# A 1024-token decoder block with PEER experts: down-projection sums over eight expert chunks instead of four

## The chip, the cores and the metric

The kernel runs on one core of one Trainium2 chip. The metric is the device time of one execution in microseconds (us), lower is better. A profiled execution gives the span from the first to the last instruction and the busy time of each engine: PE (TensorE, matrix products), DVE (VectorE), ACT (ScalarE), POOL (GpSimd) and SP (SyncE, which here only issues DMAs). 16 DMA engines move the data.

## The reference, cut to what matters

The block is an attention and convolution mixer, a layer norm, and then a PEER channel mixer with 16384 experts, which is where most of the time goes. For each of 1024 tokens, 8 heads choose 16 experts each; an expert is one row u of 1024 numbers and one row v of 1024 numbers:

```python
def chunk(args):
    xc, ec, gc = args                      # 128 tokens, their 128 experts, the gates
    u = jnp.take(u_experts, ec, axis=0)
    a = jax.nn.gelu(jnp.einsum('tkd,td->tk', u, xc), approximate=False)
    vv = jnp.take(v_experts, ec, axis=0)
    return jnp.einsum('tk,tkd->td', gc * a, vv)
# then h = layer_norm(DN_ALPHA * h + ff, ln2_g, ln2_b)
```

Summed over experts this is `(gates * gelu(h @ u.T)) @ v`, with a gate of zero for each expert that a token has not chosen.

## The kernel before, in words

The 1024 tokens are 8 blocks of 128. The experts are computed in two ways at the same time.

**Row blocks** (`ROWS`: 0, 1, 6, 7) fetch only the chosen rows. `gathered` issues, for each block, 128 indirect DMAs of u rows (L148) and 128 of v rows (L160), 128 rows of 4 KB each, so 1024 gathers of 512 KB in all. POOL issues them; they land in a pool of five buffers (`NGATHER`), shared by tag `t4k`. DVE consumes each with one instruction of 1024 columns (L150 a dot product, L162 a scaled sum in PSUM) and thereby frees the buffer.

**Dense blocks** (`DENSE`: 2 to 5, 512 tokens) compute all 16384 experts as 128 chunks (`NC`) of 128. `up(c)` loads 512 KB of u (L677), splits it into a high and a low part (ACT L120, DVE L121), runs 24 matmuls of 512 columns into one PSUM bank (L684), applies gelu on ACT (L689), multiplies by the gates on DVE (L690), and splits the product into `Wh` and `Wl`. The gates were written to DRAM earlier (`gd`); L687 fetches them for `QUAD` = 4 chunks at a time, 1 MB in pieces of 512 bytes, into two buffers `gq`. `down(q, jj)` loads 512 KB of v (L700), splits it with ACT and POOL (L121 on POOL), and for each of two slices j runs 12 matmuls (4 chunks, 3 products, L716) into a PSUM bank; DVE then adds the bank to `accT` in SBUF (L722; ACT copies it for q = 0, L720). All u and v loads go through four buffers with tag `raw`.

The loop at L755 walks the groups of chunks: first `up` of the first chunk of group q, then all the `down` steps of group q-1, then `up` of the other chunks of group q. After each of these units, `advance` traces a number of gather steps, so that all 1024 would be traced by nine tenths of the units. After the loop come the last group's `down` steps, cut into halves of 256 tokens with their layer norm (`finish`) behind each half (L773), and the remaining gathers. The framework's scheduler fixes the order of the instructions on each engine at build time from a timeline simulation, with priority by the order of the trace; on the chip each engine follows its order strictly.

Before the dense stage, mixer, routing keys and expert choice run for four pairs of blocks; some of the gathers already run there.

Of the kernel before, what the change touches and what calls it, by code (L numbers as in the profile page):

```python
# [13 lines left out]
F32 = mybir.dt.float32  # L14
F32R = mybir.dt.float32r
# [5 lines left out]
ALU = mybir.AluOpType  # L21
# [4 lines left out]
P = 128  # L26
T = 1024
D = 1024
NJ = D // P
# [16 lines left out]
ND = len(DENSE)  # L46
TD = ND * P
NMAX = max(len(g) for g in GROUPS) * P
NC = 128
QUAD = 4  # L50
TG = 32
OT = 8
HB = 64
GSCALE = 2.0 ** 15
NGATHER = 5
TK = 4
AHEAD = 8
NW = 5
EARLY = (3, 1)

WIDTH = [TOPK // (a + 1) for a in range(TOPK)]
# [16 lines left out]
def block_kernel(ctx: ExitStack, tc: tile.TileContext, d, out):  # L78
    nc = tc.nc
# [10 lines left out]
    gd = dram.tile([TD // TG, P, NC, TG], F32, name="gd")  # L90
# [92 lines left out]
    with ExitStack() as s1:  # L183
# [435 lines left out]
        n = p1.tile([P, NB, 8], F32, name="n")  # L619
# [18 lines left out]
        for gi, blocks in enumerate(GROUPS):  # L638
            x, qkv = xin
            y = p2.tile([P, NJ, NM], F32, name="y", tag="T", bufs=4)  # L640
            for b in range(2):
                a = scores(gi, b, qkv)
# [13 lines left out]
    with ExitStack() as s2:  # L656
# [15 lines left out]

        def up(c):

            q = c // QUAD
            raw = dn.tile([P, NJ, P], F32, name="uraw", tag="raw", bufs=4)
            nc.sync.dma_start(raw, d["uT"][c])  # L677
            uh = dn.tile([P, NJ, P], F32R, name="uh", tag="uh", bufs=2)
            ul = dn.tile([P, NJ, P], F32R, name="ul", tag="ul", bufs=2)
            split(uh, ul, raw)  # L680
            ps = pd.tile([P, TD], F32, name="pd")
            for j in range(NJ):
                for k, (w, z) in enumerate(((uh, 0), (uh, 1), (ul, 0))):
                    nc.tensor.matmul(ps, w[:, j], hT[z][:, j], start=(j == 0 and k == 0), stop=(j == NJ - 1 and k == 2))  # L684
            if q not in gq:
                gq[q] = dn.tile([P, TD // TG, QUAD, TG], F32, name="gq", bufs=2)
                nc.sync.dma_start(gq[q], gd[:, :, q * QUAD:(q + 1) * QUAD].rearrange("a p c t -> p a c t"))  # L687
            ge = dn.tile([P, TD], F32, name="ge", bufs=2)
            act(ge, ps, AF.Gelu)  # L689
            V.tensor_tensor(ge.rearrange("p (a t) -> p a t", t=TG), ge.rearrange("p (a t) -> p a t", t=TG),  # L690
                            gq[q][:, :, c % QUAD], op=ALU.mult)
            wh = dn.tile([P, TD], F32R, name="Wh", bufs=NW)
            wl = dn.tile([P, TD], F32R, name="Wl", bufs=NW)
            split(wh, wl, ge)
            W[c] = (wh, wl)

        def values_of(q, jj, tags=("vh", "vl")):

            raw = dn.tile([P, 2, QUAD, P], F32, name="vraw", tag="raw", bufs=4)
            nc.sync.dma_start(raw, d["vL"][q, jj])  # L700
            vh = dn.tile([P, 2, QUAD, P], F32R, name="vh", tag=tags[0], bufs=2)
            vl = dn.tile([P, 2, QUAD, P], F32R, name="vl", tag=tags[1], bufs=2)
            split(vh, vl, raw, G)
            return vh, vl

        def add(q, j, v, t0=0, n=TD):

            nonlocal accT
            if accT is None:
                accT = dn.tile([P, NJ, TD], F32, name="accT")  # L710
            vh, vl = v
            ps = pd.tile([P, n], F32, name="pd")
            for k in range(QUAD):
                wh, wl = W[q * QUAD + k]
                for p, (vv, w) in enumerate(((vh, wh), (vh, wl), (vl, wh))):
                    nc.tensor.matmul(ps, vv[:, j % 2, k], w[:, t0:t0 + n],  # L716
                                     start=(k == 0 and p == 0), stop=(k == QUAD - 1 and p == 2))
            o = accT[:, j, t0:t0 + n]
            if q == 0:
                act(o, ps, AF.Copy)  # L720
            else:
                V.tensor_tensor(o, o, ps, op=ALU.add)  # L722

        def down(q, jj):
            v = values_of(q, jj)
            for j in (2 * jj, 2 * jj + 1):
                add(q, j, v)

        def finish(b):

# [11 lines left out]
            nc.sync.dma_start(out[DENSE[b] * P:(DENSE[b] + 1) * P], h1)  # L742

        total = 2 * P * len(ROWS)
        units = NC + NC // QUAD * 4
        early = done

        def advance(u):
# [2 lines left out]
                step()  # L751

        unit = 0
        last = NC // QUAD - 1
        for q in range(last + 1):  # L755
            seq = [(up, q * QUAD)]
            if q:
                seq += [(down, q - 1, jj) for jj in range(4)]
            seq += [(up, q * QUAD + i) for i in range(1, QUAD)]
            for f, *args in seq:  # L760
                f(*args)
                next(side, None)
                unit += 1
                advance(unit)
        vs = [values_of(last, jj, ("vh", "vl") if jj < 2 else ("uh", "ul")) for jj in range(4)]
        for _ in steps:
            pass
        par = []
        for i in (2, 3):
            p = gp.tile([P, D], F32, name="ln2", tag="t4k", bufs=NGATHER)  # L770
            nc.sync.dma_start(p, ln2d[:, i:i + 1].to_broadcast([P, 1, D]).rearrange("p a e -> p (a e)"))
            par.append(p)
        for t0 in range(0, TD, 2 * P):  # L773
            for j in range(NJ):
                add(last, j, vs[j // 2], t0, 2 * P)
            for b in range(t0 // P, t0 // P + 2):
                finish(b)


def lay_out(i):  # L780
    def m(name):
        return np.asarray(i[name])
# [15 lines left out]
        "u": f(m("u_experts")[0]),  # L798
        "v": f(m("v_experts")[0]),
        "uT": f(m("u_experts")[0].reshape(NC, P, NJ, P).transpose(0, 3, 2, 1)),  # L800
        "vL": f(m("v_experts")[0].reshape(NC // QUAD, QUAD, P, NJ // 2, 2, P).transpose(0, 3, 2, 4, 1, 5)),
    }


# [10 lines left out]
```

## Time and profile before

| | us |
|---|---|
| three runs | 2740.81 to 2745.84, median 2745.84 |
| the profiled execution | 2743.4, its span 2741.6 |
| PE busy | 2290.9 (84% of the span) |
| DVE busy | 2303.3 (84%) |
| POOL busy | 1415.2 (52%) |
| ACT busy | 798.1 (29%) |
| DMA | 862.21 MB, mean 314 GB/s |

The table is a mean over three stretches with different limits: up to about 1231 us the mixer and the routing, from 1231 to 2628 us the dense stage with gathers beside it, and from 2628 us to the end gathers and the last layer norms. A share of busy time is therefore read by stretch. The time of the execution is 1.8 us longer than the span.

### The profile page before, as it was taken

Reading aid. Unit: us, or ns where it says so; the run is one execution under the profiler, and the core shown is the slowest. Engines: PE = TensorE matmul, PEld = TensorE weight load, DVE = VectorE, ACT = ScalarE, POOL = GpSimd, SP = SyncE. Lnnn points to the kernel's source line nnn. Section 1 sums busy time; section 2 is a strip of 40 time slices with the busy share of each in tenths; the row PEclk is TensorE's granted clock in tenths of the full one; section 3 lists DMA queues with packets and bytes.
Section 4 is the critical chain, followed back from the end, with each engine's and each line's share of the span. In section 5 each row is a group of like instructions: output and inputs, shape, how many; then the busy total and the mean of one; then the engine's idle time right before and its main releaser. Section 6 shows DMA issues by size and latency. Waiting matters only on the chain. (4 is left out here: it accounts for less than half of the span.)

```text
span 2741.6 us, 33269 instructions
## 1 busy us (share of the span) xinstructions
PE 2290.9 (84%) x11032; PEld 1917.8 (70%) x11032; DVE 2303.3 (84%) x4956; ACT 798.1 (29%) x1307; POOL 1415.2 (52%) x1233
## 2 busy tenths in 40 slices
PE   8999699789887622219999999999999999999940
PEld 7888587678766522218888888888888888888830
DVE  2158889999999999978888888888888888888897
ACT  2123122242443323224232322323232332323201
POOL 1000533443353344436667676666767666666753
PEclk9899799799977755559999999999999999999975
DMA  6355999899979788899999999999999999999987
GB/s 203 99 155 175 347 376 332 311 336 354 337 286 337 253 317 293 309 337 322 343 337 340 336 352 350 341 351 335 342 354 334 347 344 346 339 342 353 335 314 263
DMA packets 293900, 862.21 MB, mean 314 GB/s; under 512 B 25824, under 2 KB 97760, under 8 KB 289504
## 3 DMA queue, kind: packets, MB, share of 16 engines
q0 software_dynamic: 150480, 548.47, 54.5%
q1 hardware_dynamic: 143248, 311.62, 33.1%
q8 instruction: 87, 1.43, 0.2%
q14 instruction: 85, 0.70, 0.1%
HBM read 815.95 MB, written 44.04 MB: 314 GB/s over the span
## 5 line engine op out<-in xcount | busy, mean ns | idle before, releaser
L148 POOL DMA_INDIRECT row<-in_u,ix x512 | 532.9, 1041 | 586.7 <-DVE row L150 242.9
L160 POOL DMA_INDIRECT row<-in_v,ix x512 | 554.8, 1084 | 474.4 <-DVE pg L162 229.9
L162 DVE SCALAR_TENSOR_TENSOR pg<-row,a,pg 128x1024 f32<-128x1024 f32 x512 | 656.4, 1282 | 33.8 <-DMA row<-in_v,ix 27.8
L684 PE MATMUL pd<-hT,uh 128*128 128x512 f32 x2048 | 635.8, 390 | 42.8 <-ACT uh L120 42.8
L150 DVE SCALAR_TENSOR_TENSOR row<-row,pg 128x1024 f32<-128x1024 f32 x512 | 611.7, 1212 | 45.4 <-DMA row<-in_u,ix 44.8
L684 PEld LDWEIGHTS pd<-hT,uh 128*128 128x128 f32 x2048 | 385.4, 188 | 123.0 <-ACT uh L120 43.0
L716 PE MATMUL pd<-Wl,vh 128*128 128x512 f32 (+1 forms) x1056 | 402.3, 383 | 0.0
L684 PE MATMUL pd<-hT,ul 128*128 128x512 f32 x1024 | 399.3, 390 | 0.0
L716 PE MATMUL pd<-Wh,vh 128*128 128x512 f32 (+1 forms) x1056 | 397.4, 383 | 0.2 <-ACT Wh L120 0.2
L716 PE MATMUL pd<-Wh,vl 128*128 128x512 f32 (+1 forms) x1056 | 392.1, 383 | 0.3 <-POOL vl L121 0.3
L121 POOL TENSOR_TENSOR vl<-vraw,vh 128x1024 fp32r<-128x1024 f32 x128 | 309.4, 2417 | 72.7 <-ACT vh L120 68.6
L267 PE MATMUL pk<-o,oh 128*128 128x128 f16 x512 | 109.2, 277 | 208.2 <-DVE oh L261 131.3
L370 PE MATMUL mm<-x,raw 128*128 128x256 f32 x1152 | 269.2, 386 | 13.1 <-DMA x<-in_xT 7.7
L120 ACT ACTIVATE vh<-vraw 128x1024 fp32r<-128x1024 f32 x128 | 135.9, 1062 | 455.7 <-PE pd L716 302.1
L722 DVE TENSOR_TENSOR accT<-accT,pd 128x512 f32<-128x512 f32 (+1 forms) x256 | 169.4, 667 | 109.8 <-PE pd L716 97.8
L370 PEld LDWEIGHTS mm<-x,raw 128*128 128x128 f32 x1152 | 215.8, 193 | 45.2 <-issue 8.1
L370 PE MATMUL mm<-h,raw 128*128 128x256 f32 x1024 | 238.1, 385 | 1.5 <-ACT h L539 1.0
L716 PEld LDWEIGHTS pd<-Wh,vl 128*128 128x128 f32 x1056 | 198.4, 188 | 39.3 <-POOL vl L121 0.7
L716 PEld LDWEIGHTS pd<-Wl,vh 128*128 128x128 f32 x1056 | 198.5, 188 | 38.9 <-DVE Wl L121 0.2
L716 PEld LDWEIGHTS pd<-Wh,vh 128*128 128x128 f32 x1056 | 198.0, 188 | 39.2 <-ACT Wh L120 0.4
L121 DVE TENSOR_TENSOR ul<-uraw,uh 128x1024 fp32r<-128x1024 f32 x128 | 159.7, 1248 | 76.1 <-ACT uh L120 70.8
L684 PEld LDWEIGHTS pd<-hT,ul 128*128 128x128 f32 x1024 | 192.8, 188 | 40.9 <-DVE ul L121 0.8
(211 smaller groups left out, 2756.0 us busy)
## 6 DMA issues: line engine op xcount, KB each, us to landing
raw<-in_wall SPq DMA_DIRECT2D x168, 512.0 KB
uraw<-in_uT SPq DMA_DIRECT2D x128, 512.0 KB
vraw<-in_vL SPq DMA_DIRECT2D x128, 512.0 KB
gd<-st SPq DMA_DIRECT2D x32, 1024.0 KB
gq<-gd SPq DMA_DIRECT2D x32, 1024.0 KB
row<-in_u,ix POOLq DMA_INDIRECT x512
row<-in_v,ix POOLq DMA_INDIRECT x512
x<-in_xT SPq DMA_DIRECT2D x16, 256.0 KB
```

The source lines that it names most:

```text
L120: act(dh, src, AF.Copy)
L121: eng.tensor_tensor(dl, src, dh.bitcast(F32), op=ALU.subtract)
L148: G.indirect_dma_start(out=row, out_offset=None, in_=d["u"], in_offset=bass.IndirectOffsetOnAxis(ap=idx[tb][:, k:k + 1], axis=0))
L150: V.scalar_tensor_tensor(row, row, 1.0, h1p, op0=ALU.mult, op1=ALU.mult, accum_out=a[:, k:k + 1])
L160: G.indirect_dma_start(out=row, out_offset=None, in_=d["v"], in_offset=bass.IndirectOffsetOnAxis(ap=idx[tb][:, k:k + 1], axis=0))
L162: V.scalar_tensor_tensor(acc, row, a[:, k:k + 1], acc, op0=ALU.mult, op1=ALU.add)
L267: nc.tensor.matmul(ps[:, t], oh[:, :, t2 + t], o1[:, t2 + t], start=True, stop=False)
L370: nc.tensor.matmul(ps[:, :n], w[:, j], mov[:, j, :n], start=(j == 0), stop=(j == NJ - 1))
L684: nc.tensor.matmul(ps, w[:, j], hT[z][:, j], start=(j == 0 and k == 0), stop=(j == NJ - 1 and k == 2))
L716: nc.tensor.matmul(ps, vv[:, j % 2, k], w[:, t0:t0 + n], start=(k == 0 and p == 0), stop=(k == QUAD - 1 and p == 2))
L722: V.tensor_tensor(o, o, ps, op=ALU.add)
```

## The change

Groups are of eight chunks (`OCT`) instead of four. One `down(q, j)` covers a single slice j of eight chunks: the same 512 KB of v and the same 24 matmuls as a `down(q, jj)` before, but in one PSUM sum instead of two, so that `accT` is touched once for eight chunks. There are still 128 `up` and 128 `down` units. The nine `Wh`/`Wl` buffers (`NW`) replace five. The gates are fetched for eight chunks, 2 MB in pieces of 1 KB, into one buffer instead of two. The last group's `down` steps run over all 512 tokens, before the rest of the gathers in the trace, and the four `finish` steps follow; the halves of 256 tokens and the use of the `uh`/`ul` buffers for v are gone. The SBUF area for the descriptors of POOL's DMAs is set to 8192 bytes. The layout of `vL` in DRAM follows.

```diff
--- before.py
+++ after.py
@@ -47,15 +47,16 @@
 TD = ND * P
 NMAX = max(len(g) for g in GROUPS) * P
 NC = 128
-QUAD = 4
+OCT = 8
 TG = 32
 OT = 8
 HB = 64
 GSCALE = 2.0 ** 15
 NGATHER = 5
+SCRATCH = 8192
 TK = 4
 AHEAD = 8
-NW = 5
+NW = 9
 EARLY = (3, 1)
 
 WIDTH = [TOPK // (a + 1) for a in range(TOPK)]
@@ -672,7 +673,7 @@
 
         def up(c):
 
-            q = c // QUAD
+            q = c // OCT
             raw = dn.tile([P, NJ, P], F32, name="uraw", tag="raw", bufs=4)
             nc.sync.dma_start(raw, d["uT"][c])
             uh = dn.tile([P, NJ, P], F32R, name="uh", tag="uh", bufs=2)
@@ -683,48 +684,46 @@
                 for k, (w, z) in enumerate(((uh, 0), (uh, 1), (ul, 0))):
                     nc.tensor.matmul(ps, w[:, j], hT[z][:, j], start=(j == 0 and k == 0), stop=(j == NJ - 1 and k == 2))
             if q not in gq:
-                gq[q] = dn.tile([P, TD // TG, QUAD, TG], F32, name="gq", bufs=2)
-                nc.sync.dma_start(gq[q], gd[:, :, q * QUAD:(q + 1) * QUAD].rearrange("a p c t -> p a c t"))
+                gq[q] = dn.tile([P, TD // TG, OCT, TG], F32, name="gq")
+                nc.sync.dma_start(gq[q], gd[:, :, q * OCT:(q + 1) * OCT].rearrange("a p c t -> p a c t"))
             ge = dn.tile([P, TD], F32, name="ge", bufs=2)
             act(ge, ps, AF.Gelu)
             V.tensor_tensor(ge.rearrange("p (a t) -> p a t", t=TG), ge.rearrange("p (a t) -> p a t", t=TG),
-                            gq[q][:, :, c % QUAD], op=ALU.mult)
+                            gq[q][:, :, c % OCT], op=ALU.mult)
             wh = dn.tile([P, TD], F32R, name="Wh", bufs=NW)
             wl = dn.tile([P, TD], F32R, name="Wl", bufs=NW)
             split(wh, wl, ge)
             W[c] = (wh, wl)
 
-        def values_of(q, jj, tags=("vh", "vl")):
-
-            raw = dn.tile([P, 2, QUAD, P], F32, name="vraw", tag="raw", bufs=4)
-            nc.sync.dma_start(raw, d["vL"][q, jj])
-            vh = dn.tile([P, 2, QUAD, P], F32R, name="vh", tag=tags[0], bufs=2)
-            vl = dn.tile([P, 2, QUAD, P], F32R, name="vl", tag=tags[1], bufs=2)
+        def values_of(q, j):
+
+            raw = dn.tile([P, OCT, P], F32, name="vraw", tag="raw", bufs=4)
+            nc.sync.dma_start(raw, d["vL"][q, j])
+            vh = dn.tile([P, OCT, P], F32R, name="vh", bufs=2)
+            vl = dn.tile([P, OCT, P], F32R, name="vl", bufs=2)
             split(vh, vl, raw, G)
             return vh, vl
 
-        def add(q, j, v, t0=0, n=TD):
+        def add(q, j, v):
 
             nonlocal accT
             if accT is None:
                 accT = dn.tile([P, NJ, TD], F32, name="accT")
             vh, vl = v
-            ps = pd.tile([P, n], F32, name="pd")
-            for k in range(QUAD):
-                wh, wl = W[q * QUAD + k]
+            ps = pd.tile([P, TD], F32, name="pd")
+            for k in range(OCT):
+                wh, wl = W[q * OCT + k]
                 for p, (vv, w) in enumerate(((vh, wh), (vh, wl), (vl, wh))):
-                    nc.tensor.matmul(ps, vv[:, j % 2, k], w[:, t0:t0 + n],
-                                     start=(k == 0 and p == 0), stop=(k == QUAD - 1 and p == 2))
-            o = accT[:, j, t0:t0 + n]
+                    nc.tensor.matmul(ps, vv[:, k], w,
+                                     start=(k == 0 and p == 0), stop=(k == OCT - 1 and p == 2))
+            o = accT[:, j]
             if q == 0:
                 act(o, ps, AF.Copy)
             else:
                 V.tensor_tensor(o, o, ps, op=ALU.add)
 
-        def down(q, jj):
-            v = values_of(q, jj)
-            for j in (2 * jj, 2 * jj + 1):
-                add(q, j, v)
+        def down(q, j):
+            add(q, j, values_of(q, j))
 
         def finish(b):
 
@@ -742,7 +741,7 @@
             nc.sync.dma_start(out[DENSE[b] * P:(DENSE[b] + 1) * P], h1)
 
         total = 2 * P * len(ROWS)
-        units = NC + NC // QUAD * 4
+        units = NC + NC // OCT * NJ
         early = done
 
         def advance(u):
@@ -751,18 +750,19 @@
                 step()
 
         unit = 0
-        last = NC // QUAD - 1
+        last = NC // OCT - 1
         for q in range(last + 1):
-            seq = [(up, q * QUAD)]
+            seq = [(up, q * OCT)]
             if q:
-                seq += [(down, q - 1, jj) for jj in range(4)]
-            seq += [(up, q * QUAD + i) for i in range(1, QUAD)]
+                seq += [(down, q - 1, j) for j in range(NJ)]
+            seq += [(up, q * OCT + i) for i in range(1, OCT)]
             for f, *args in seq:
                 f(*args)
                 next(side, None)
                 unit += 1
                 advance(unit)
-        vs = [values_of(last, jj, ("vh", "vl") if jj < 2 else ("uh", "ul")) for jj in range(4)]
+        for j in range(NJ):
+            down(last, j)
         for _ in steps:
             pass
         par = []
@@ -770,11 +770,8 @@
             p = gp.tile([P, D], F32, name="ln2", tag="t4k", bufs=NGATHER)
             nc.sync.dma_start(p, ln2d[:, i:i + 1].to_broadcast([P, 1, D]).rearrange("p a e -> p (a e)"))
             par.append(p)
-        for t0 in range(0, TD, 2 * P):
-            for j in range(NJ):
-                add(last, j, vs[j // 2], t0, 2 * P)
-            for b in range(t0 // P, t0 // P + 2):
-                finish(b)
+        for b in range(ND):
+            finish(b)
 
 
 def lay_out(i):
@@ -798,12 +795,12 @@
         "u": f(m("u_experts")[0]),
         "v": f(m("v_experts")[0]),
         "uT": f(m("u_experts")[0].reshape(NC, P, NJ, P).transpose(0, 3, 2, 1)),
-        "vL": f(m("v_experts")[0].reshape(NC // QUAD, QUAD, P, NJ // 2, 2, P).transpose(0, 3, 2, 4, 1, 5)),
+        "vL": f(m("v_experts")[0].reshape(NC // OCT, OCT, P, NJ, P).transpose(0, 3, 2, 1, 4)),
     }
 
 
 def kernel(**inputs):
-    nc = bacc.Bacc("TRN2", target_bir_lowering=False, num_devices=1)
+    nc = bacc.Bacc("TRN2", target_bir_lowering=False, num_devices=1, dynamic_dma_scratch_size=SCRATCH)
     arrays = {f"in_{k}": a for k, a in lay_out(inputs).items()}
     d = {k[3:]: nc.dram_tensor(k, a.shape, mybir.dt.from_np(a.dtype), kind="ExternalInput").ap()
          for k, a in arrays.items()}
```

## Rows read from the trace of the kernel before

**Rows 1.** Busy time by stretch: us, five engines (count), PE clock, DMA share, GB/s.
```profile
0.00:1231.00 1231.00, 889.77 (x4761) 754.77 (x4762) 1021.45 (x3338) 356.66 (x750) 421.04 (x459) 0.81 0.80 286
1231.00:2628.00 1397.00, 1396.47 (x6234) 1158.58 (x6234) 1188.27 (x1502) 432.01 (x539) 942.85 (x718) 1.00 0.95 341
2628.00:2742.00 114.00, 4.65 (x41) 4.41 (x39) 93.59 (x118) 9.47 (x18) 51.34 (x56) 0.53 0.81 290
```

**Rows 2.** PE's waits, 1231 to 2628 us: total us, times, longest.
```profile
PE pd L684 <- ACT uh L120: 42.8, 1, 42.8
PE pd L716 <- POOL vl L121: 0.3, 1, 0.3
```

**Rows 3.** Gathers by stretch, POOL busy (count): L148, then L160 twice.
```profile
1231.00:2628.00 1397.00, 276.99 (x256) 1.00 0.95 341
...
1231.00:2628.00 1397.00, 350.84 (x324) 1.00 0.95 341
2628.00:2742.00 114.00, 49.69 (x53) 0.53 0.81 290
```

**Rows 4.** DVE in order of time near the end: start, us, what, idle before.
```profile
2631.20 0.41 DVE L722 TENSOR_TENSOR accT<-accT,pd 128x256 f32<-128x256 f32 x1
...
2712.62 2.61 DVE L162 SCALAR_TENSOR_TENSOR pg<-row,a,pg 128x1024 f32<-128x1024 f32 x2 [0.72 <-DMA row<-in_v,ix]
...
2736.38 1.28 DVE L117 SCALAR_TENSOR_TENSOR h1f<-h1f,lnst,ln 128x1024 f32<-128x1024 f32 x1
```

**Rows 5.** DMA queues, 2640 to 2710 us: packets, MB, share of 16 engines.
```profile
q0 software_dynamic: 6600, 24.03, 95.9%
```

**Rows 6.** DVE's waits, 1231 to 2628 us: total us, times, longest.
```profile
DVE accT L722 <- PE pd L716: 97.8, 128, 2.2
...
DVE pg L162 <- DMA row<-in_v,ix: 15.1, 19, 2.0
...
DVE row L150 <- DMA row<-in_u,ix: 9.2, 12, 2.1
```

**Rows 7.** POOL's waits, 1231 to 2628 us.
```profile
POOL row L160 <- DVE pg L162: 161.5, 147, 13.1
POOL row L148 <- DVE row L150: 105.1, 104, 2.8
...
POOL row L160 <- issue: 37.9, 130, 2.1
```

**Rows 8.** Groups by line: busy us, mean ns of one, idle before.
```profile
L162 DVE SCALAR_TENSOR_TENSOR pg<-row,a,pg 128x1024 f32<-128x1024 f32 x512 | 656.4, 1282 | 33.8 <-DMA row<-in_v,ix 27.8 <-DVE accT L722 0.7 <-ACT pg L157 0.6
...
L722 DVE TENSOR_TENSOR accT<-accT,pd 128x512 f32<-128x512 f32 x240 | 163.3, 685 | 109.5 <-PE pd L716 97.6 <-issue 11.3
```

**Rows 9.** DMA queues, 1782 to 1798 us, with packets by size.
```profile
DMA packets 3417, 5.96 MB, mean 373 GB/s; under 512 B 169, under 2 KB 2217, under 8 KB 3417
...
q1 hardware_dynamic: 2484, 2.58, 48.9%
```

**Rows 10.** DMA queues, 1231 to 2628 us.
```profile
q0 software_dynamic: 84942, 309.30, 58.7%
q1 hardware_dynamic: 98952, 166.25, 36.0%
```

**Rows 11.** SP's waits, 1231 to 2628 us.
```profile
SPq L687 <- DVE ge L690: 71.9, 30, 5.2
```

**Rows 12.** SP's DMA issues in order of time.
```profile
1199.48 10.07 SPq L687 DMA_DIRECT2D gq<-gd  x2
1212.06 20.15 SPq L677 DMA_DIRECT2D uraw<-in_uT  x5
...
1782.20 0.38 SPq L687 DMA_DIRECT2D gq<-gd  x1
```

**Rows 13.** ACT in order of time.
```profile
1229.55 1.06 ACT L120 ACTIVATE uh<-uraw 128x1024 fp32r<-128x1024 f32 x1 [10.57 <-DMA uraw<-in_uT]
```

**Rows 14.** DVE in order of time.
```profile
1230.64 1.22 DVE L121 TENSOR_TENSOR ul<-uraw,uh 128x1024 fp32r<-128x1024 f32 x1 [9.01 <-ACT uh L120]
```

## Prediction

> **What bounds the kernel now.** I read the table of stretches first, because the shares over the whole span mix three regimes [rows 1]. Up to 1231 us the change touches nothing. From 1231 to 2628 us PE is busy 1396.47 of 1397 us at a granted clock of 1.00, and its list of waits holds one wait at the stage's start and one of 0.3 us [rows 2]: this stretch lasts as long as its 6144 matmuls of 512 columns, 1397 / 6144 = 0.227 us each, 5.46 us for a unit of 24. From 2628 us PE is idle, and only gathers and layer norms are left. The reader is to see there that PE being full does not make PE the only bound: 256 + 324 = 580 gathers were issued inside the dense stage and 53 after it [rows 3]. DVE's order near the end shows it: the last sum into `accT` is done at 2631.6, the last gathered row is consumed at 2715.2, and the last layer norm ends at 2737.7 [rows 4]. So the end is 84 us of leftover gathers, then some 26 us of norms and stores.
>
> What sets the pace of the gathers? In the dense stage the DMA engines are busy 95% of the time at 341 GB/s [rows 1]. With gathers alone, from 2640 to 2710 us, queue q0 fills 95.9% of the engines and moves 24.03 MB in 70 us, 343 GB/s, or 1.53 us for a gather of 0.524 MB [rows 5]. Both stretches run near the same limit. But in the dense stage DVE stands for a gathered row only 15.1 + 9.2 us in all [rows 6], and POOL often stands until DVE frees a row buffer, 161.5 + 105.1 us [rows 7]. So there the fixed order of DVE, POOL and PE paces the gathers, a little below what DMA could carry: 5% of 1397 us, 70 us of DMA time, is unused.
>
> **The change, part by part.** *PE.* There are 6144 products of the same shape (the last group's halves of 256 columns become full ones, the same columns). No price for opening a sum shows, since units of 24 and of 12 matmuls run through without a gap [rows 2]. I take 0; bounds -2 and +2 us.
>
> *Sums into accT.* Before, 240 full adds and 16 of half width; after, 15 groups of 8, 120 full adds. At 0.685 us each [rows 8] the 120 that go are 82 us of DVE, and the halves some 6 more. The waits of these adds for PE, 97.8 us in 128 times [rows 6], should fall to about half, another 49 us. None of this lies on PE's path, so by itself it is worth 0. It is room: a gather needs about 1.28 us of DVE [rows 8], and the 58 gathers that are left or in flight at 2628 us need 74 us.
>
> *Gates.* A stretch with one fetch of gates shows its 2048 pieces of 512 bytes (2217 packets under 2 KB less 169 under 512 B), and q1 takes 48.9% of 16 us, 7.8 us, for 2.58 MB [rows 9]. The other 1.53 MB of it, at the pace of q0 in the dense stage, 309.30 MB in 58.7% of 1397 us or 377 GB/s [rows 10], take 4.1 us, so one fetch costs 3.7 us of all engines and 32 cost 120 us; a piece is 29.4 ns. A 4 KB packet at 377 GB/s on 16 engines is 174 ns; on the straight line between the two a piece of 1 KB is 50 ns. The 16 new fetches, again of 2048 pieces, then cost 102 us: 18 us of DMA time saved. Bounds: 0 if time goes by bytes, 31 us if 1 KB runs at 377 GB/s (33.55 MB in 89 us). I take 18, since both ends of the line are rows. The Trainium skill ("DMA: Bandwidth & Descriptors", Specifications) puts the size from which transfers run at line rate at 512 bytes. By it nothing is saved here, and the sum below would be 18 us higher; the trace, with 3.7 us for 1.05 MB against 2.8 us at 377 GB/s, does not agree.
>
> *One buffer of gates.* The fetch for group q now waits on SP until DVE has multiplied the last chunk of group q-1; with two buffers SP already stood 71.9 us in 30 such waits [rows 11], a group earlier. Queued behind it on SP are the u and v loads. Four `raw` buffers and two split pairs lie ahead of PE; v loads 2 to 5 are issued before the fetch, and the next one has some 18 us before its split is due (four `down` units less 3.5 us of splitting), so PE is covered as long as the fetch takes less. How long it takes: at least 2.1 MB at 377 GB/s, 5.6 us; at most about 20 us, since at the start two 1 MB fetches were issued by 1209.5 and the u load issued behind them at 1212.06 was used at 1229.55 [rows 12, 13]. The gates are first wanted 6 us after their issue (one `up` of PE, then gelu). So the multiply of the group's first chunk can be 0 to 14 us late, at 15 boundaries. Its result is not needed until eight `down` units later, 43 us, so it costs nothing if the scheduler placed it late enough in DVE's order, and much if it did not (below). I take 0.5 us a boundary, 8 us, nearer the lower end because PE's waits in the steady stage are 0.3 us in all [rows 2].
>
> *Runs of eight.* Eight `up` units in a row ask DVE for more than eight `down` units do. Over a group the work is less than before; I take 0, with 50 us more tail as the far end (two gathers fewer in each of 16 groups, 32 x 1.53).
>
> *The end.* The first two `finish` steps lose their early start; their two DVE passes of about 0.67 us each now come later, but under the gathers. I take +2 us, bounds 0 and +10. *Descriptor area halved, and the memory layout:* POOL's issue gaps before v gathers are 37.9 us in 130 times [rows 7], 0.3 us each, and POOL is busy 943 of 1397 us [rows 1]; even doubled they fit. I take 0. The stage's start may move by its own load wait, 9 us either way [rows 14].
>
> *The sum.* Leftover gathers go at 1.53 us for each that is moved into the dense stage. The 18 us of saved DMA time carry 12 of them; of the 70 us of unused DMA time I let DVE's new room use a third, 23 us, 15 gathers (bounds 0 and all, up to 84 us together, where the tail is gone). From the profiled execution, 2743.4 us: -18 - 23 + 8 + 2 = -31, so **2712 us**. The median of the runs shown, 2745.84, is 2.4 us above the profiled execution; I make no correction for that.
>
> **The rivals.** *All leftover gathers fit.* If DVE's work was what paced them, its 88 + 49 us of new room holds all 74 us. Then the norms follow PE: 2631.6 + 26 us of norms and stores + 1.8 us outside the span, with a little slack, **2663 us**. For it: POOL waits for DVE and not for data [rows 7]. Against it: it needs 18 + 66 us of DMA time, all that there is.
>
> *No change.* The change doesn't do what it says for the time: the scheduler's order holds the same number of gathers per unit, because in its plan DMA was the limit and the pieces' size is no matter, so 58 gathers remain after PE and end as before: **2743 us**. For it: 341 and 343 GB/s in the two stretches [rows 1, 5]. Here the skill's rule on 512 bytes would put it too.
>
> *Slower: the gates stop DVE.* DVE follows its order strictly. If the multiply is placed as if the fetch took 6 us and it takes 16, DVE stands 10 us at each boundary. Such a stop is in the trace: at the dense start, behind two fetches of gates, DVE stood 9.01 us for a u load [rows 14]. A stopped DVE frees no row buffer, POOL stands at its next gather, and the split of v queued behind that gather on POOL comes late, so PE waits. That split is due on average half to one unit later, so about 5 of the 10 us reach PE: 15 x 5 = 75 us, 2743.4 - 18 + 75 = **2800 us**. It decides from 2.7 us a boundary on (41 / 15). For it: one buffer, twice the data, 6 us of time. Against it: the order can hide it, and the saved adds let DVE catch up. By the skill's sentence that each DMA engine goes round its queue rows packet by packet (same page, "Queues, rings and completion order"), 128 pieces an engine would each wait for a 174 ns gather packet, 26 us for a fetch before and 29 us now; the fetch of [rows 9], issued at 1782.20 [rows 12] and wholly moved by 1798, took at most 16, so the trace does not bear that out at its full price.
>
> **How the numbers follow.** Chances: forecast (about 2699 to 2737) 0.40, all fit 0.12, no change 0.13, slower 0.35. Faster by over 0.2% 0.52, within 0.2% (about what a measurement of this kernel can tell from no change, 5.5 us) 0.13, slower 0.35. The range leaves out some 0.1 on each side: 2665 at the low end, where nearly all gathers fit, and 2795 at the high end, near the full price of the stops. The likeliest sign's own range is 2665 to 2737.
>
> **What would show it.** Right: fewer than 58 rows consumed after PE's last product, some 31; half the adds of L722 and about half their wait; PE without waits through the stage; the gates' fetches down to about 102 us of DMA time. Wrong: waits of PE for POOL's split of v, and of DVE's L690 for `gq`, once in 87 us; or as many gathers after PE as now.

## The result and the profile after

The changed kernel takes 2855.97 us (median of four runs, 2851.19 to 2863.9) where the kernel before takes 2745.84: a ratio of 1.0408, 95% interval 1.0377 to 1.0438. It is slower by 4%. The forecast, 2712 us, had the wrong sign, and the time lies above the range; the rival that came about is the last one, "the gates stop DVE", and it cost more than the 2800 us at which it was priced.

The profiled execution took 2863.9 us, the longest of the four; its span is 2862.1 us, 120.5 us more than before, so its losses below add up to some 10 us more than the medians differ by. The lines of the changed file stand one lower: L684 is now L685 (`up` product), L716 is L717 (`down` product), L690 is L691 (gates), L687 is L688 (fetch of gates), L722 is L723 (sum into `accT`), L121 and L120 are L122 and L121 (splits), L148 to L162 are L149 to L163.

First the dense stage, from PE's first to its last product (us, busy us and count of PE, PEld, DVE, ACT and POOL, granted PE clock, DMA share, GB/s), after:

```profile
1234.90:2755.70 1520.80, 1441.45 (x6158) 1177.84 (x6159) 1174.95 (x1369) 423.38 (x539) 961.14 (x723) 0.96 0.89 315
```

and the same stretch of the kernel before, cut at its own first and last product:

```profile
1230.70:2630.90 1400.20, 1399.67 (x6258) 1161.78 (x6259) 1191.47 (x1506) 432.01 (x539) 944.65 (x720) 1.00 0.95 341
```

The stage starts 4.2 us later, is 120.6 us longer, and what follows it is 106.4 us instead of 110.7 (to the spans' ends): the whole loss is in the dense stage. PE is idle in it for 1520.8 - 1441.45 = 79.4 us, before 0.5; and it is busy 41.8 us longer, for the same products, at a mean granted clock of 0.96. The waits after, 1231 to 2862 us (total us, times, longest), say who was late [rows 2, 6]:

```profile
DVE ge L691 <- DMA gq<-gd: 141.6, 15, 12.3
DVE accT L723 <- PE pd L717: 102.4, 51, 4.9
```

```profile
PE pd L717 <- POOL vl L122: 48.2, 18, 5.7
PE pd L685 <- ACT uh L121: 40.6, 1, 40.6
PE pd L717 <- ACT vh L121: 30.4, 11, 4.2
```

The first row did not exist before. Fifteen times, once for each group behind the first, DVE stands for the gates, 9.4 us in the mean, and PE pays with 48.2 + 30.4 us of waits for the split of v (the 40.6 us are the stage's start, 42.8 before). One such boundary in order of time (start, us, engine, line, what; idle before it and who ended that) shows the path:

```profile
1944.96 0.38 SPq L688 DMA_DIRECT2D gq<-gd  x1
...
1950.94 0.68 DVE L723 TENSOR_TENSOR accT<-accT,pd 128x512 f32<-128x512 f32 x1
1963.39 0.69 DVE L691 TENSOR_TENSOR ge<-ge,gq 128x512 f32<-128x512 f32 x1 [11.77 <-DMA gq<-gd]
...
1950.56 1.06 ACT L121 ACTIVATE vh<-vraw 128x1024 fp32r<-128x1024 f32 x1 [2.85 <-PE pd L717]
1964.12 0.63 ACT L121 ACTIVATE Wh<-ge 128x512 fp32r<-128x512 f32 x1 [12.50 <-DVE ge L691]
1964.65 1.99 ACT L121 ACTIVATE vh<-vraw 128x1024 fp32r<-128x1024 f32 x2
...
1965.77 2.37 POOL L122 TENSOR_TENSOR vl<-vraw,vh 128x1024 fp32r<-128x1024 f32 x1 [11.11 <-ACT vh L121]
...
1965.75 0.50 PE L717 MATMUL pd<-Wh,vh 128*128 128x512 f32 x1 [4.17 <-ACT vh L121]
1968.19 0.79 PE L717 MATMUL pd<-Wh,vl 128*128 128x512 f32 x1 [1.71 <-POOL vl L122]
```

SP issues the fetch at 1944.96. DVE's order asks for the gates 6.7 us later, and they are used 18.4 us after the issue; DVE does nothing in between. ACT's next instruction is the copy of that product into `Wh`, and queued behind it on ACT is the split of the next v; POOL waits for that, PE for both. This path, through ACT, is that of six of the fifteen boundaries. In eight others POOL stands at a gather until DVE frees a row buffer, with the split of v queued behind it, as here (DVE stood 9.15 us at this one; in the boundary left over, POOL's gather waited for ACT and PE for ACT's split):

```profile
2544.58 0.94 POOL L149 DMA_INDIRECT row<-in_u,ix  x1 [9.98 <-DVE row L151]
...
2549.20 0.79 PE L717 MATMUL pd<-Wh,vl 128*128 128x512 f32 x1 [5.03 <-POOL vl L122]
```

The table of stretches around the first boundary (columns as above) shows what else stops:

```profile
1955.00:1961.00 6.00, 6.00 (x29) 4.95 (x28) 0.00 (x0) 0.00 (x0) 0.00 (x0) 1.00 1.05 381
1961.50:1966.00 4.50, 0.33 (x2) 0.25 (x2) 1.91 (x3) 1.88 (x3) 0.23 (x1) 1.00 0.15 58
1966.00:1970.00 4.00, 2.29 (x6) 1.53 (x6) 3.93 (x5) 0.64 (x1) 3.55 (x3) 0.56 0.12 32
1970.00:1974.00 4.00, 4.00 (x12) 3.12 (x11) 3.75 (x4) 0.00 (x0) 3.37 (x4) 0.58 0.96 354
1974.00:1978.00 4.00, 4.00 (x20) 3.28 (x19) 2.48 (x4) 1.06 (x1) 3.51 (x4) 1.00 0.96 341
```

With DVE stopped no row buffer comes free, so once the gathers in flight are done the DMA engines stand idle as well (shares of 0.15 and 0.12). And when PE comes back after its idle time its granted clock is 0.56 to 0.58, close to the lower of its two levels, 1.2 of 2.4 GHz, for some 8 us: 12 products in 4 us instead of 20. Such stretches make up most of the 41.8 us of longer busy time, 2.8 a boundary; 4.4 us of it is there without the stops too (e1 below).

The leftover gathers, the place where the forecast looked for its gain, did not move. Rows of v consumed in the three stretches (us, DVE busy and count, clock, DMA share, GB/s; u rows are all done before the stage ends), after and then before:

```profile
0.00:1234.90 1234.90, 166.10 (x130) 0.81 0.80 285
1234.90:2755.70 1520.80, 423.17 (x330) 0.96 0.89 315
2755.70:2863.00 107.30, 67.47 (x53) 0.53 0.80 289
```

```profile
1230.70:2630.90 1400.20, 419.43 (x327) 1.00 0.95 341
2630.90:2742.00 111.10, 71.31 (x56) 0.52 0.81 292
```

### The profile page after: what moved, and what is told of

Same layout as the page of the kernel before. It is cut to its first block, busy times and chain, and to the rows that moved or that the text cites. A ratio compares the mean times of both kernels' runs of the same rounds, so it can differ in the third digit from the quotient of the medians.

```text
span 2862.1 us, 32900 instructions
## 1 busy us (share of the span) xinstructions
PE 2334.1 (82%) x10936; PEld 1935.5 (68%) x10936; DVE 2284.1 (80%) x4820; ACT 789.3 (28%) x1307; POOL 1426.9 (50%) x1233
## 5 line engine op out<-in xcount | busy, mean ns | idle before, releaser
L149 POOL DMA_INDIRECT row<-in_u,ix x512 | 528.0, 1031 | 659.6 <-DVE row L151 294.4
L161 POOL DMA_INDIRECT row<-in_v,ix x512 | 570.3, 1114 | 483.7 <-DVE pg L163 249.4
L163 DVE SCALAR_TENSOR_TENSOR pg<-row,a,pg 128x1024 f32<-128x1024 f32 x512 | 656.7, 1283 | 46.3 <-DMA row<-in_v,ix 37.7
L685 PE MATMUL pd<-hT,uh 128*128 128x512 f32 x2048 | 632.4, 390 | 40.6 <-ACT uh L121 40.6
L685 PEld LDWEIGHTS pd<-hT,uh 128*128 128x128 f32 x2048 | 385.3, 188 | 120.7 <-ACT uh L121 40.8
L717 PE MATMUL pd<-Wh,vl 128*128 128x512 f32 x1024 | 415.6, 406 | 48.4 <-POOL vl L122 48.2
L717 PE MATMUL pd<-Wh,vh 128*128 128x512 f32 x1024 | 413.7, 404 | 30.9 <-ACT vh L121 30.4
L717 PE MATMUL pd<-Wl,vh 128*128 128x512 f32 x1024 | 411.0, 401 | 0.0
L685 PE MATMUL pd<-hT,ul 128*128 128x512 f32 x1024 | 399.2, 390 | 0.0
L122 POOL TENSOR_TENSOR vl<-vraw,vh 128x1024 fp32r<-128x1024 f32 x128 | 310.5, 2426 | 97.7 <-ACT vh L121 95.4
L717 PEld LDWEIGHTS pd<-Wh,vl 128*128 128x128 f32 x1024 | 200.6, 196 | 101.4 <-POOL vl L122 58.8
L717 PEld LDWEIGHTS pd<-Wh,vh 128*128 128x128 f32 x1024 | 201.1, 196 | 77.8 <-ACT vh L121 35.4
L121 ACT ACTIVATE uh<-uraw 128x1024 fp32r<-128x1024 f32 x128 | 135.6, 1059 | 411.2 <-PE pd L685 290.7
L122 DVE TENSOR_TENSOR ul<-uraw,uh 128x1024 fp32r<-128x1024 f32 x128 | 191.5, 1496 | 49.4 <-ACT uh L121 45.1
L717 PEld LDWEIGHTS pd<-Wl,vh 128*128 128x128 f32 x1024 | 200.5, 196 | 42.8
L685 PEld LDWEIGHTS pd<-hT,ul 128*128 128x128 f32 x1024 | 192.6, 188 | 40.8 <-DVE ul L122 0.8
L272 ACT ACTIVATE st<-pk 128x256 f32<-128x256 f32 x256 | 137.0, 631 | 291.3 <-PE pk L269 206.3
```

Source lines behind the costliest of these rows:

```text
L121: act(dh, src, AF.Copy)
L122: eng.tensor_tensor(dl, src, dh.bitcast(F32), op=ALU.subtract)
L149: G.indirect_dma_start(out=row, out_offset=None, in_=d["u"], in_offset=bass.IndirectOffsetOnAxis(ap=idx[tb][:, k:k + 1], axis=0))
L161: G.indirect_dma_start(out=row, out_offset=None, in_=d["v"], in_offset=bass.IndirectOffsetOnAxis(ap=idx[tb][:, k:k + 1], axis=0))
L163: V.scalar_tensor_tensor(acc, row, a[:, k:k + 1], acc, op0=ALU.mult, op1=ALU.add)
L272: act(st[z][:, :, tt:tt + 4].rearrange("p n t -> p t n"), ps[:, :, z * 64:(z + 1) * 64], AF.Copy, scale=1.0 / GSCALE)
```

## The experiments

**e1: groups of eight, gates for four.** The first theory (A in what was expected) is that the late gates cost the 110 us; this kernel is the changed one with the fetch of before.

```diff
-            q = c // OCT
+            q = c // 4
-                gq[q] = dn.tile([P, TD // TG, OCT, TG], F32, name="gq")
-                nc.sync.dma_start(gq[q], gd[:, :, q * OCT:(q + 1) * OCT]...)
+                gq[q] = dn.tile([P, TD // TG, 4, TG], F32, name="gq", bufs=2)
+                nc.sync.dma_start(gq[q], gd[:, :, q * 4:(q + 1) * 4]...)
```

> Sums of eight chunks stay, the gates are fetched as before: four chunks, 512-byte pieces, two buffers. Theory A (the late gates stop DVE and through it PE): no wait of DVE for gq, PE's waits in the dense stage fall from 79 us to under 5 us, the time returns to 2735 to 2750 us. Rival B (runs of eight up and eight down units run out of split and load buffers, whatever the gates do): PE keeps most of its 79 us of waits and the time stays at 2820 to 2860 us.

Measured: 2754.45 us, ratio 1.0025 (1.0012 to 1.0038), 4 us above the range of theory A. No wait for `gq` is left, and the dense stage is

```profile
1235.90:2649.50 1413.60, 1404.03 (x6158) 1157.80 (x6159) 1164.49 (x1370) 426.25 (x539) 969.38 (x724) 1.00 0.95 339
```

107 of the 121 us are gone with the fetch alone. What else was changed keeps 13.4 us of loss in the stage: 9.6 us in which PE is idle (seven waits for POOL's split of v, at most 2.6 us; under 5 us were expected) and 4.4 us of busy time. It gains nothing in return.

**e2: the old groups of four, gates for eight.** The same suspect alone, in the kernel before.

```diff
-            q = c // QUAD
+            q = c // 8
-                gq[q] = dn.tile([P, TD // TG, QUAD, TG], F32, name="gq", bufs=2)
+                gq[q] = dn.tile([P, TD // TG, 8, TG], F32, name="gq")
```

> The kernel before with only the gates changed: eight chunks, 1 KB pieces, one buffer; sums of four chunks stay. Theory A: DVE stands some 9 us for gq at each of 15 boundaries, PE waits 50 us or more, 2800 to 2860 us. Rival B: the runs of four are kept, so PE waits under 5 us and the time is 2735 to 2755 us.

Measured: 2794.69 us, ratio 1.0170 (1.0141 to 1.0200). DVE stands as it does in the changed kernel, nearly, and PE about half as long:

```profile
DVE ge L690 <- DMA gq<-gd: 114.4, 15, 11.4
```

```profile
PE pd L684 <- DVE ul L121: 14.2, 8, 4.0
PE pd L716 <- POOL vl L121: 13.9, 12, 2.5
PE pd L716 <- ACT vh L120: 4.1, 2, 2.1
```

Theory A had wanted 50 us or more of PE's waits and at least 2800 us, its rival under 5 us and at most 2755: the measured values lie between, nearer to A. The fetch by itself makes the kernel slower, so the wait comes from it and not from the groups of eight. But a stop of 7.6 us costs here 50.2 us of stage (36.2 idle, 14.6 of longer busy time), not 107: how much reaches PE hangs on what stands around the stop in the orders. The single buffer and the doubled fetch were not tried apart.

**e3: the changed kernel, the first multiply of each group later.** The cause is left, and its place in DVE's order is changed: the multiply and the split behind it are traced behind the sum of the fourth `down` (for the first group boundary they stay where they were).

```diff
+            if c % OCT == 0 and c > OCT:
+                held.append((c, ge))
+            else:
+                gate(c, ge)
...
-                V.tensor_tensor(o, o, ps, op=ALU.add)
+                i = V.tensor_tensor(o, o, ps, op=ALU.add)
+                if held and j == 3:
+                    with tc.issue_after(i.ins):
+                        gate(*held.pop())
```

> The changed kernel, but the gate multiply and split of each group's first chunk are put behind the fourth down unit's add on DVE, some 22 us later; fetch, pieces and buffer are unchanged. Theory A, with the point that only the multiply's place in DVE's order does the harm: no wait of DVE for gq, PE's waits under 10 us, 2725 to 2750 us. Rival B: PE's waits stay near 79 us, 2820 to 2860 us. If the single buffer itself starved the loads behind it on SP, PE would wait for v or u loads and the time would be in between.

Measured: 2752.72 us, ratio 1.0017 (1.0003 to 1.0032), 3 us above the range of theory A; the dense stage is 1413.7 us, that of e1. DVE waits for the gates once, 10.5 us, at the boundary that was left, and PE stands 4.3 us there. So one buffer and 2 MB a fetch are harmless where the product is not asked for early; the order, not the transfer, makes the stop. e1 and e3 differ in the size of the gates' pieces, too. Queue q1 (packets, MB, share of 16 engines) over the stages of e1, e3 and e2:

```profile
q1 hardware_dynamic: 98977, 166.35, 34.8%
```

```profile
q1 hardware_dynamic: 68018, 166.37, 34.0%
```

```profile
q1 hardware_dynamic: 67971, 166.21, 33.2%
```

34.8% of 1413.6 us less 34.0% of 1413.7 are 11 us of DMA time less with pieces of 1 KB; the other pair, the kernel before (36.0% of 1397 us [rows 10]) and e2 (33.2% of 1450.4), gives 21 us. But before and e1 differ by 11 us as well, with pieces of the same size, so the amount is not settled. Neither the stage nor the rows in it (331 of v in e1, 330 in e3) show any of it.

**e4: the changed kernel without ACT in the path.** In the boundary above ACT carries the stop to PE, which the prediction had not named. Here DVE makes the first `Wh` of each group.

```diff
-            split(wh, wl, ge)
+            if c % OCT == 0 and c:
+                V.tensor_copy(wh, ge)
+                V.tensor_tensor(wl, ge, wh.bitcast(F32), op=ALU.subtract)
+            else:
+                split(wh, wl, ge)
```

> The changed kernel, but for each group's first chunk DVE instead of ACT makes the copy Wh from ge, so that nothing on ACT waits for the late multiply. DVE should still stand some 9 us at 15 boundaries in either case. Route through ACT (Wh holds up the next split of v on ACT): PE's waits fall from 79 us to under 25 us and the time to 2745 to 2790 us. Route through POOL (the prediction's: no row buffer comes free, so the split of v queued behind a gather is late): PE's waits stay over 60 us, 2830 to 2860 us.

Measured: 2867.87 us, ratio 1.0430 (1.0404 to 1.0456), no gain, and 8 us above the range given for the route through POOL. The waits of PE in the stage:

```profile
PE pd L721 <- POOL vl L122: 94.5, 17, 10.6
PE pd L685 <- ACT uh L121: 39.2, 1, 39.2
PE pd L721 <- ACT vh L121: 0.7, 2, 0.5
```

ACT's share, 30.4 us, went to 0.7, and POOL's grew from 48.2 to 94.5. So the path through POOL's gathers can carry the whole stop by itself. It does not follow that the path through ACT cost nothing in the changed kernel: POOL's order is another one here. At the boundary shown above POOL went straight on to the split of v; in e4 it stands there 12.94 us at a gather placed ahead of that split, and PE 8.49 us behind it. To cut one path alone is not enough, as the stop takes the other.

**e5: no gates after the first group.** Groups 1 to 15 use the gates of group 0, so 15 of the 16 fetches, 31 MB, are left out, and with them the right gates of 15 groups. It asks whether bytes or DVE's work set how many rows fit into the stage.

```diff
-            if q not in gq:
+            if not gq:
-                            gq[q][:, :, c % OCT], op=ALU.mult)
+                            gq[0][:, :, c % OCT], op=ALU.mult)
```

> The changed kernel with the gates fetched once only: groups 1 to 15 use the gates of group 0 (15 of 16 fetches are left out, 31 MB). There is nothing late for DVE to wait for, so theory A wants PE's waits under 10 us and the dense stage near 1414 us. The open question is why DVE's and DMA's freed time took no more gathers: if the plan of the order, or the chip, was short of DMA, the 31 MB make room for some 60 gathers, the rows consumed after PE's last product fall from 53 to under 20 and the time to 2660 to 2700 us. If the five row buffers (the round of a gather: issue, landing, DVE) set the number per unit, 45 to 58 rows remain and the time is 2735 to 2755 us.

Measured: 2686.86 us, ratio 0.9784 (0.9762 to 0.9806). No row of v is left behind the stage, and the bytes of the stage (packets, MB, mean, packets by size) are those of before, shown behind it:

```profile
1224.30:2660.90 1436.60, 490.70 (x382) 0.99 0.93 332
2660.90:2685.00 24.10, 0.00 (x0) 0.64 0.25 98
...
DMA packets 130767, 476.93 MB, mean 332 GB/s; under 512 B 14524, under 2 KB 14524, under 8 KB 130681
```

```profile
DMA packets 184187, 477.39 MB, mean 341 GB/s; under 512 B 14076, under 2 KB 75516, under 8 KB 184100
```

The order fills the stage to the same 477 MB: 31 MB of gates out, 55 rows of 0.524 MB, 29 MB, in. DVE takes those 55 rows; the stage is 23 us longer than that of e1, a quarter of the tail that goes, and PE waits 21.9 us in it, where under 10 were expected. So bytes set the number of rows that the fixed order holds, not DVE's work, and neither fewer sums (e1 and e3: 479 and 480 MB) nor the size of the gates' pieces changes it much. The planner's own rule was not looked at; that it counts bytes is read from these sums.

**e6, e7: six row buffers.** e6 is the kernel before with `NGATHER = 6`, e7 is e3 with `NGATHER = 6`.

```diff
-NGATHER = 5
+NGATHER = 6
```

> The kernel before with six row buffers instead of five and nothing else. Row buffers set the pace: the rows after PE's last product fall from 56 to under 25 and the time to 2680 to 2720 us. DMA sets it: 50 or more remain, 2735 to 2755 us.

> The changed kernel with the late multiply and six row buffers. With the 88 us of DVE time freed and a buffer more: if row buffers set the pace, under 20 rows remain and the time is 2670 to 2710 us; if DMA sets it, 45 to 58 remain and it stays at 2740 to 2760 us.

Measured: e6 2717.25 us, ratio 0.9900 (0.9878 to 0.9921); e7 2719.05 us, 0.9908 (0.9885 to 0.9932). e6's time lies in the range of the first theory, but its rows do not bear it out: 40 of v remain behind the stage, neither under 25 nor 50, the stage holds 328 (327 before), and the gain is 15 more rows ahead of it, 145. e7, between its two ranges, holds 336 in the stage, 33 behind, and its stage is 16 us longer than e6's. On top of six buffers, too, the groups of eight bring nothing.

**e8: the descriptor area alone.** The kernel before, with the smaller area.

```diff
+SCRATCH = 8192
...
-    nc = bacc.Bacc("TRN2", target_bir_lowering=False, num_devices=1)
+    nc = bacc.Bacc("TRN2", target_bir_lowering=False, num_devices=1, dynamic_dma_scratch_size=SCRATCH)
```

> The kernel before with only the descriptor area of POOL's DMAs cut to 8192 bytes. I priced this at 0: 2740 to 2752 us, POOL's gather unchanged. If the smaller area held gathers back, the gathers' mean of 1.04 and 1.08 us on POOL or the issue waits would grow and the time with them.

Measured: 2747.83 us, ratio 1.0004 (0.9990 to 1.0019): nothing.

**e9, e11: smaller doses of the stop.** e3 with the multiply behind the sum of the second (e9) and the third (e11) `down`.

```diff
-                if held and j == 3:
+                if held and j == 1:
```

> A half dose of the stop. The changed kernel with the first gate multiply of each group (and the split behind it) traced behind the add of the second `down` instead of the fourth: one PE unit of 5.5 us later than in the changed kernel, where DVE stood 9.4 us a boundary. Theory A (the stop of DVE reaches PE through the row buffers and POOL, in proportion, less what the two v loads ahead cover): DVE's wait for `gq` falls to 3 to 6 us a boundary, 45 to 90 us in all; PE stands under 25 us in the dense stage instead of 79, since most of a stop this long is covered; the time is 2755 to 2790 us. Rival (a threshold: anything over 2.7 us a boundary, as the prediction had it, passes half of itself to PE): PE stands 25 to 45 us and, with the half clock behind it, the time is 2790 to 2830 us. If DVE's wait is under 2 us a boundary, the fetch is shorter when DVE does not stand, and the time is that of the fourth `down`, 2753 us.

> A small dose: the first gate multiply of each group traced behind the add of the third `down`. With the second `down` DVE asked for the gates some 12 us after their issue, they were there after 18 to 20 us, DVE stood 7.1 us a boundary, PE 4.5 us of it, and the dense stage was 1506 us. Theory B (a stop passes to PE a fixed share, some 0.55 of itself, at any size, and half-clock stretches of PE behind it): asked 17 to 18 us after the issue, DVE stands 1 to 2.5 us a boundary, 15 to 38 us in all; PE stands 8 to 20 us in the dense stage after its start, and the dense stage is 1422 to 1445 us, the time 2762 to 2785 us. Rival (the buffers ahead of PE and of POOL cover a stop this small; the cost begins above it): PE stands as in the fourth `down`'s kernel, 9.5 us, no half-clock stretch more, the dense stage is 1411 to 1419 us, the time 2748 to 2758 us.

Measured: e9 2836.13 us, ratio 1.0325 (1.0300 to 1.0351), above both expectations; e11 2758.95 us, 1.0039 (1.0025 to 1.0054), between them. In e9 DVE's waits for the gates are 106.9 us, 7.1 a boundary, and PE's for the split of v 66.0. A boundary of e9 shows the path through POOL undisturbed by ACT (PE's waits for ACT's split are 1.9 us in all there):

```profile
1952.28 0.69 DVE L699 TENSOR_TENSOR ge<-ge,gq 128x512 f32<-128x512 f32 x1 [7.24 <-DMA gq<-gd]
...
1954.44 1.14 POOL L161 DMA_INDIRECT row<-in_v,ix  x1 [6.74 <-DVE pg L163]
...
1958.53 2.35 POOL L122 TENSOR_TENSOR vl<-vraw,vh 128x1024 fp32r<-128x1024 f32 x1
...
1960.93 0.79 PE L725 MATMUL pd<-Wh,vl 128*128 128x512 f32 x1 [5.29 <-POOL vl L122]
```

POOL stands 6.74 us at a gather for a buffer, issues it and two more, and only then splits v, 5.29 us too late for PE. The kernels in order of PE's idle time in the dense stage:

| kernel | DVE's wait for gates, us (times) | PE idle | PE busy | stage | median us |
|---|---|---|---|---|---|
| before | none | 0.5 | 1399.67 | 1400.2 | 2745.84 |
| e1 | none | 9.6 | 1404.03 | 1413.6 | 2754.45 |
| e3, fourth `down` | 10.5 (1) | 9.7 | 1404.00 | 1413.7 | 2752.72 |
| e11, third | 29.7 (10) | 15.5 | 1404.89 | 1420.4 | 2758.95 |
| e2 | 114.4 (15) | 36.2 | 1414.25 | 1450.4 | 2794.69 |
| e9, second | 106.9 (15) | 68.1 | 1438.37 | 1506.5 | 2836.13 |
| changed | 141.6 (15) | 79.4 | 1441.45 | 1520.8 | 2855.97 |
| e4 | 131.6 (14), and 10.9 at one that the trace puts down to ACT | 95.3 | 1434.20 | 1529.5 | 2867.87 |

From e3 to e11, 19.2 us more of waits, 2.1 in the mean of nine, pass 5.8 us to PE, a third; from e3 to e9, 96.4 us more pass 58.4, three fifths. My theory that what lies ahead of PE covers most of a stop of 7 us fell: what POOL has queued ahead of the split adds to the delay as it comes back. Why e2 passes on half of what e9 does at the same wait is open; its largest part, 14.2 us, takes a third path, the split of u on DVE itself.

**e10: seven row buffers.** The kernel before with the smaller descriptor area and `NGATHER = 7`.

```diff
-NGATHER = 5
+NGATHER = 7
+SCRATCH = 8192
...
+    nc = bacc.Bacc("TRN2", target_bir_lowering=False, num_devices=1, dynamic_dma_scratch_size=SCRATCH)
```

> The kernel before with seven row buffers instead of five, paid for by the descriptor area of 8192 bytes. With six buffers the time was 2717 us: 15 more rows were taken in ahead of the dense stage, and none inside it. Theory A (a buffer brings rows ahead of the dense stage and lets the tail run closer to the DMA's pace; the dense stage itself is paced by the order's plan, 582 rows): 5 to 15 more rows before the dense stage, 580 to 590 inside it, 25 to 35 after it, 2695 to 2717 us. Rival (buffers pace the dense stage): over 600 rows in it and under 2690 us. If six buffers already gave all there is, 2717 us again.

Measured: 2693.96 us, ratio 0.9814 (0.9793 to 0.9835), the fastest of the complete kernels here and 1 us under the range of theory A. Rows of v by stretch:

```profile
0.00:1241.70 1241.70, 213.41 (x167) 0.81 0.82 299
1241.70:2642.90 1401.20, 420.80 (x328) 1.00 0.95 343
2642.90:2693.00 50.10, 21.92 (x17) 0.56 0.59 220
```

37 rows more than before ahead of the dense stage, one more in it, 39 fewer behind it. From six buffers to seven 22 rows more came ahead of it, where 5 to 15 were expected, and 17 remain behind it, where 25 to 35 were. A row buffer pays in the stretch before the dense stage, where the DMA engines have room (a share of 0.80 [rows 1]), and not in the stage that is full.

## Why the prediction was wrong

**Where it was right.** The bound: the dense stage is paced by PE and carries all the bytes it can, and the end by leftover rows. The sums: L722 and L723 fell from 168.9 to 81.3 us in the stage, 87.6 us, against the 88 forecast. The descriptor area at nothing (e8's ratio 1.0004). PE's sums at nothing, nearly: e1's busy time is 4.4 us longer, past the bound of 2, and the granted clock is 0.79 and 0.80 in the 8 us behind its two longest waits, so the sums need not be what costs it. The start, 4.2 us late, is inside its 9. The rival's working held in its sizes: asked for some 6 us after the issue, a stop of 10 us (9.4 measured), "about 5 of the 10 us reach PE" (79.4 / 15 = 5.3). Its path, by the buffer, the gather and the split of v on POOL, is that of eight of the fifteen boundaries (and of e4 and e9); in the others the stop went through ACT, which the rival did not name, so that the sum came out so close is in part luck.

**The step that failed: the wait for the gates.** The prediction bounded the wait at 0 to 14 us a boundary, and took 0.5, 8 us in all; DVE in fact stood 9.4 us in the mean of 15 boundaries, 141.6 us, and PE 79.4 us in the stage. The prediction put its value "nearer the lower end because PE's waits in the steady stage are 0.3 us". That row [rows 2] was no evidence: it is of a kernel with two buffers, in which the gates were never waited for. The row that applied was the one that the prediction took as its upper end, the 20 us behind the fetches at the stage's start [rows 12, 13]: boundaries of the changed kernel have 16.0 to 19.6 us from issue to use. The condition on which the low value hung, that the multiply stands late in DVE's order, was not borne out by its place in the code, ahead of the `down` steps; DVE asked 4 to 14 us behind the issue. e3 and e1 take that wait away in two ways and both come within 0.3% of the kernel before.

**The rival's size.** 75 us were priced, and the stage lost 120.6. The idle time, 79.4 us, is the 75; the longer busy time of 41.8 us, most of it the lower clock behind the stops, was not in the sum, and the 18 us that it took off for the gates' pieces did not come.

**The gain that was not there.** The sum had 12 rows from cheaper packets and 15 from DVE's room. Packets: 18 us of DMA time were forecast, 11 (e1 against e3) and 21 (before against e2) are measured, and kernels with the same pieces differ by 11, so the 18 are neither confirmed nor refuted; but no row moved, and the time is as if nothing were saved. By the Trainium skill's figure ("DMA: Bandwidth & Descriptors", Specifications: line rate from 512 bytes on), which the prediction set aside, it would be nothing; these traces do not decide it. Room: in e1, where no stop is, 331 rows of v are in the stage, 327 before. e5 shows why: the order holds 477 to 480 MB (before, e1, e3, e5), whatever DVE does. This is the "no change" rival's mechanism, and without the stop its time, 2743 us, would have been right within 0.5% (e1 and e3). The halving of DVE's waits for sums, 97.8 us, did not come either: 102.4, in 51 instead of 128 times.

**Runs of eight** were taken at nothing, with 50 us as the far end: e1 shows 13.4 us in the stage, 9.1 as waits of PE for v and 4.4 as busy time, less 5 us in the tail. e3's 13.5 us hold the one stop that was left, so there it is less. No run parts the length of the runs from the other differences of the order. The end was taken at +2 us; it is 4.3 us shorter, of which the three rows fewer behind PE, at 1.53 us each, explain 4.6, so +0.3 is left for the change itself.

## What to carry to other kernels

A buffer dropped and a transfer doubled are priced from issue to use in the trace, under the load of that stage, and set against the place in the order where the data is first asked for; a zero wait in a kernel with the second buffer says nothing of one without it. An engine with a strict order that stops for something not urgent stops whoever is queued behind it: move the request, not the transfer. And before time on one engine is counted as room, check what the planner fills the stage by, here bytes.

## What the hardware showed beyond that

**Most of DVE's freed time went back into other instructions.** DVE's busy time in the stage fell by 16.5 us (1191.47 to 1174.95), not by the 87.6 of the sums. Groups by line (count, busy us, mean ns) after:

```profile
L122 DVE TENSOR_TENSOR ul<-uraw,uh 128x1024 fp32r<-128x1024 f32 x128 | 191.5, 1496 | 49.4 <-ACT uh L121 45.1 <-issue 3.4
L122 DVE TENSOR_TENSOR Wl<-ge,Wh 128x512 fp32r<-128x512 f32 x128 | 134.6, 1052 | 12.5 <-ACT Wh L121 12.1
L723 DVE TENSOR_TENSOR accT<-accT,pd 128x512 f32<-128x512 f32 x119 | 81.3, 684 | 104.8 <-PE pd L717 102.4 <-issue 2.0
```

and before:

```profile
L121 DVE TENSOR_TENSOR ul<-uraw,uh 128x1024 fp32r<-128x1024 f32 x128 | 159.7, 1248 | 76.1 <-ACT uh L120 70.8 <-issue 3.0 <-PE pd L684 1.8
L121 DVE TENSOR_TENSOR Wl<-ge,Wh 128x512 fp32r<-128x512 f32 x128 | 92.5, 723 | 0.7 <-ACT Wh L120 0.7
```

For the same 128 splits each, 31.8 and 42.1 us are lost. Two of them in order of time, with what POOL does then:

```profile
2119.16 2.41 POOL L122 TENSOR_TENSOR vl<-vraw,vh 128x1024 fp32r<-128x1024 f32 x1
...
2119.61 2.52 DVE L122 TENSOR_TENSOR Wl<-ge,Wh 128x512 fp32r<-128x512 f32 x1
...
2126.17 0.68 DVE L122 TENSOR_TENSOR Wl<-ge,Wh 128x512 fp32r<-128x512 f32 x1
```

The one that begins inside POOL's split of v ends 0.56 us after it, 2.52 us in all; the one beside no split takes 0.68. Over the kernel the `Wl` splits that overlap a split of POOL take 2.73 us in the mean (23 of 128), the others 0.684; of before only 8 overlap. The sums into `accT`, with one input in PSUM, take 0.68 us with or without overlap; 104 of them lay beside a split of POOL before, 25 after, so it seems that with half of them gone the order put more of the sensitive instructions there. The Trainium skill ("SBUF — State Buffer", Who interferes with whom) has this as a port shared by a DVE instruction with two SBUF inputs and a GpSimd instruction that reads SBUF; the trace agrees.

**The clock.** Behind boundaries where PE stood, it came back at a granted clock of about half (0.56 and 0.58 above), and 41.8 us of the loss, a third, is longer busy time. In e9 it is 38.7 us, behind 68.1 us of idle time. In e2, whose 36.2 us of idle time are cut into shorter waits (the longest is 4.0 us), it is 14.6.
